# A hybrid mixer block with 32 experts on one core: adaLN sums on VectorE alone, a ninth weight slot, work taken out of the first expert pair, and another order for the last expert pair's down weights

## The chip, the cores and the metric

The kernel runs on one core of one Trainium2 chip. TensorE (PE) does matrix products into PSUM; VectorE (DVE), ScalarE (ACT) and GpSimd (POOL) do elementwise work; SyncE (SP) issues nearly all DMA loads, in the order of its own queue. The metric is device microseconds of one whole run.

## The reference, cut to what matters

One layer on 256 tokens of width 1024, all in float32:

```python
mod = silu(c) @ w_ada + b_ada                         # 1024 x 6144; shift1, scale1, gate1, shift2, scale2, gate2
h = rms_norm(x, g_mix) * (1 + scale1) + shift1
z = h @ w_in                                          # feeds four token mixers and 4 x 1024 merge logits
up_n = y_n @ w_branch[n]                              # y_n: MoBA, GLA, retention, sliding window; 256 wide
mixed = sum_n(sigmoid(merge_logits_n) * up_n) @ w_out
x = x + gate1 * mixed
h2 = rms_norm(x, g_ffn) * (1 + scale2) + shift2
logits = h2 @ w_router + b_router                     # top 4 of 32, softmax over the four
for e in range(32):                                   # every expert's weights are read: 12 MB each
    gu = h2 @ w_gate_up[e] + b_gate_up[e]             # 1024 x 2048
    act = clamped_swiglu(gu)
    y += combine[:, e] * (act @ w_down[e] + b_down[e])  # 1024 x 1024
x = rms_norm(x + gate2 * y, g_final)
```

## The kernel before, in words

**The front.** `ada(s_, j)` (L235) forms one half (512 columns) of one of the six rows of `mod`: two 1 MB loads bring 8 tiles of 128x512; the first four are multiplied by a column of silu(c) on ACT (L249; on POOL, L247, for row 2), added on POOL (L251), and the other four are multiplied and added on DVE (L254). The steps are dealt out one by one among the other work (`slow_step`). `z = h @ w_in` is made in units of 256 columns: `z_unit` splits each float32 weight tile of 128x512 into a high part (ACT, L347) and the rest (DVE, L348), and TensorE multiplies three of the four products of parts (L361, 48 matmuls a unit). The low parts sit in a pool of WP=4 tiles. The last 16 units are the merge units: each also multiplies a mixer's output by a piece of w_branch (`pu`, L809, 12 matmuls), takes a sigmoid, a product (L816) and a sum into `mix` (L817, partly on POOL). The output projection (`pw`, L765) follows; w_out is first multiplied by gate1 on POOL (L774). Then come the logits: x1 is transposed, multiplied by the router (L873, result transposed), copied and turned back by a second set of matmuls (L896); then the top 4 (L905 to L909), the places of the tokens (`pos`), and `gather` (L982 to L1010), which picks each expert's up to 64 tokens by a selection matrix `pm`.

**The experts.** They are taken in pairs, four to a group. `gate_up(e)` reads four 2 MB tiles `wg` (L1067, 64 matmuls of 512 columns), swiglu follows on ACT and DVE, `down(e)` reads two 2 MB tiles `wd` (L1094), and `scatter` multiplies the pair's result back to the tokens' places (`py`, L1104). In pair 0, `down_bias` (L957 to L973: the 32 b_down rows weighted for every token, `pyb`) and the transposes of `spread` (`psm`, L1032, fed by POOL's `pc`, L1024) stand between the two downs. For the last pair, `last_down` loads both experts' w_down by blocks of columns, 256 (three times) and 128 (twice) wide, expert 30's and 31's for each block, and finishes each block at once (`pdl`, L1128; `ol`; `pyl`, L1135; `x_sb`, L1137), so that the final norm is nearly done when the last weights arrive.

**What sets the order.** All loads stand in SP's queue in program order. `slot` deals them out over a ring of 2 MB slots: 5, and 3 more from the third merge branch on; a load waits until its slot's former contents have been read, and everything behind it on SP waits with it. Half slots (1 MB) are dealt by `wtile`. The engines run their own queues in order; a scheduler chose the order in each.

Of the kernel before, what the change touches and what calls it, by code (L numbers as in the profile page):

```python
# [42 lines left out]
def hybrid_block_kernel(ctx, tc, x, c, w_ada, b_ada, g_norm_mix, w_in, w_gla_gate, b_gla_gate, g_gla_norm,  # L43
# [191 lines left out]
    def ada(s_, j):  # L235
        w = []
        for i in range(2):
            t = wtile(f"wada{s_}_{j}{i}").rearrange("p (k f) -> p k f", f=512)
            nc.sync.dma_start(t, w_ada[0, i * 512:(i + 1) * 512, s_ * D + j * 512:s_ * D + (j + 1) * 512].rearrange(
                "(k p) f -> p k f", p=P))  # L240
            w += [t[:, k, :] for k in range(4)]
        acc = acs[s_, j] = mp.tile([P, 512], F32, tag="acs", name=f"acs{s_}{j}", bufs=1)
# [16 lines left out]
    def ada_end(s_, j):
        while slow:  # L260
            slow_step()
        acc = acs.pop((s_, j))
        pt = bank("t", f"pmt{s_}{j}")
        for kk in range(4):
            T.transpose(pt[:, kk * P:(kk + 1) * P], chan(acc, kk) if s_ in (3, 4) else acc[:, kk * P:(kk + 1) * P],
                        ident)
        col = cp.tile([P, 4], F32, tag="ade", name=f"ade{s_}{j}")
        V.tensor_reduce(col, pt.rearrange("p (k r) -> p k r", k=4), AX.X, ALU.add)
        V.tensor_tensor(modT[:, s_, 4 * j:4 * j + 4], col, bT[:, s_, 4 * j:4 * j + 4], ALU.add)
# [1051 lines left out]
```

## Time and profile before

| | us |
|---|---|
| median of 3 runs (lowest, highest) | 1263.29 (1259.78, 1267.72) |
| the profiled execution's own time | 1264.25 |
| its span in the trace | 1262.5 |
| front, up to the first gather matmul | 314.4 |
| from there to the last update of x | 937.6 |
| final norm and output | 10.5 |

Busy over the span: PE 93%, DVE 38%, ACT 16%, POOL 10%. The core moved 469.88 MB, 372 GB/s on average and 428 GB/s in the long middle. A busy PE is modelled from pipelined matmuls, so a high share doesn't say that it ran at its peak; the number of instructions in a stretch tells more.

### The profile page before, as it was taken

How to read it: one execution, taken by the hardware profiler on the slowest of the kernel's cores; microseconds unless marked ns; L12 is line 12 of the kernel's file. 1: busy time of each engine (PE TensorE's matmuls, PEld its weight loads, DVE VectorE, ACT ScalarE, POOL GpSimd, SP SyncE). 2: the span in 40 equal slices, each digit the busy share in tenths (PEclk: the TensorE clock that was granted, in tenths of full speed). 3: DMA queues.
4: the chain of work that ended last, by engine and by line, in shares of the span. 5: the costliest groups of instructions: out<-in, count | busy, mean ns of one | idle time of the engine just before them, and what ended most of it. 6: DMA issues, size and time to landing. Idle time of an engine off the chain costs nothing.

```text
span 1262.5 us, 14878 instructions
## 1 busy us (share of the span) xinstructions
PE 1172.2 (93%) x6204; PEld 567.7 (45%) x6204; DVE 484.4 (38%) x833; ACT 204.8 (16%) x403; POOL 131.2 (10%) x171
## 2 busy tenths in 40 slices
PE   7999999989999999999999999999989998989875
PEld 4778798987333433333333333333323332332224
DVE  3797598986342312222222223222212222132123
ACT  3458355445100000000000000000000000000001
POOL 2332213740000000000000000000000000000001
PEclk9999899999999999999999999999999999999999
DMA  9975369947889999999999999999999999999994
GB/s 324 337 248 201 133 221 341 346 160 276 320 365 396 429 427 429 427 427 428 428 428 428 428 428 428 426 428 427 429 427 428 427 428 428 428 427 428 427 382 145
DMA packets 74730, 469.88 MB, mean 372 GB/s; under 512 B 6425, under 2 KB 27010, under 8 KB 50594
## 3 DMA queue, kind: packets, MB, share of 16 engines
q1 hardware_dynamic: 74034, 467.64, 90.6%
q10 hardware_dynamic: 624, 1.23, 0.3%
q8 instruction: 50, 0.82, 0.3%
q14 instruction: 22, 0.18, 0.0%
HBM read 467.81 MB, written 1.05 MB: 371 GB/s over the span
## 4 chain that ended last, share of the span: by engine, by line
PE 61%; DMA 23%; DVE 10%; issue 2%; ACT 1%; POOL 1%; ACTq 0%; SPq 0%; POOLq 0%; DVEq 0%
DMA wd<-in_w_down_dram 13%; PE ed L1094 13%; PE ea L1067 12%; PE eb L1067 12%; DMA wg<-in_w_gate_up_dram 9%; PE pz_m L361 5%; PE py L1104 4%; PE pg L1000 2%; PE pw L765 2%; PE pu L809 1%; PE pdl L1128 1%; DMA wada<-in_w_ada_dram 1%; PE eat L1081 1%; DVE el L1045 1%; DVE el L1047 1%
## 5 line engine op out<-in xcount | busy, mean ns | idle before, releaser
L1067 PE MATMUL ea<-wg,he 128*64 128x512 f32 x1024 | 284.9, 600 | 8.9 <-DMA wg<-in_w_gate_up_dram 8.7
L1067 PE MATMUL eb<-wg,he 128*64 128x512 f32 x1024 | 283.6, 593 | 0.0
L1094 PE MATMUL ed<-wd,aT 128*64 128x512 f32 x960 | 214.6, 598 | 9.5 <-DMA wd<-in_w_down_dram 8.3
L1041 DVE TENSOR_SCALAR eg<-ea 128x512 f32<-128x512 f32 x32 | 22.1, 692 | 356.6 <-PE ea L1067 352.5
L1043 ACT ACTIVATE es<-eg 128x512 f32<-128x512 f32 x32 | 20.2, 630 | 827.9 <-DVE eg L1041 827.9
L1067 PEld LDWEIGHTS eb<-wg,he 128*64 128x64 f32 x1024 | 80.2, 137 | 146.9 <-issue 146.8
L1067 PEld LDWEIGHTS ea<-wg,he 128*64 128x64 f32 x1024 | 72.9, 137 | 145.6 <-issue 119.4
L1094 PEld LDWEIGHTS ed<-wd,aT 128*64 128x64 f32 x960 | 67.4, 137 | 143.8 <-issue 126.9
L1024 POOL TENSOR_TENSOR pc<-pm,comb 128x128 f32<-128x128 f32 x64 | 23.5, 402 | 685.2 <-PE psm L1032 624.3
L361 PE MATMUL pz_m<-hh,wl_m 128*128 128x256 f32 x256 | 73.3, 286 | 5.9 <-DVE wl_m L348 5.8
L361 PE MATMUL pz_m<-hh,wh_m 128*128 128x256 f32 x256 | 73.6, 287 | 0.0
L361 PE MATMUL pz_m<-hl,wh_m 128*128 128x256 f32 x256 | 72.1, 282 | 0.0
L1106 DVE TENSOR_TENSOR x_sb<-x_sb,py 128x512 f32<-128x512 f32 x60 | 41.3, 688 | 30.3 <-PE py L1104 30.3
L361 PEld LDWEIGHTS pz_m<-hh,wl_m 128*128 128x128 f32 x256 | 49.0, 191 | 8.0 <-DVE wl_m L348 7.7
L1104 PE MATMUL py<-oa,sm 128*128 128x512 f32 x60 | 33.8, 645 | 19.4 <-DVE oa L1098 19.4
L361 PEld LDWEIGHTS pz_m<-hl,wh_m 128*128 128x128 f32 x256 | 49.1, 192 | 0.1
L361 PEld LDWEIGHTS pz_m<-hh,wh_m 128*128 128x128 f32 x256 | 49.0, 191 | 0.3
L1097 DVE TENSOR_TENSOR oa<-ed,late 64x512 f32<-64x512 f32 x15 | 10.2, 683 | 94.6 <-PE ed L1094 94.6
L1097 DVE TENSOR_TENSOR ob<-ed,late 64x512 f32<-64x512 f32 x15 | 10.2, 682 | 91.0 <-PE ed L1094 91.0
L348 DVE TENSOR_TENSOR wl_m<-win_m,wh_m 128x512 fp32r<-128x512 f32 x44 | 42.0, 971 | 7.0 <-ACT wh_m L347 6.9
L1058 PE MATMUL ea<-bgu,ident 32*64 32x512 f32 x128 | 36.5, 612 | 0.0
L1081 PEld LDWEIGHTS eat<-ident,el 128*128 128x128 f32 x128 | 17.6, 205 | 41.0 <-DVE el L1047 39.3
(450 smaller groups left out, 1567.8 us busy)
## 6 DMA issues: line engine op xcount, KB each, us to landing
wg<-in_w_gate_up_dram SPq DMA_DIRECT2D x128, 2048.0 KB, 26.7
wd<-in_w_down_dram SPq DMA_DIRECT2D x60, 2048.0 KB, 27.0
wada<-in_w_ada_dram SPq DMA_DIRECT2D x13, 1024.0 KB, 7.4
win_m<-in_w_in_dram SPq DMA_DIRECT2D x11, 1024.0 KB
win_c<-in_w_in_dram SPq DMA_DIRECT2D x8, 1024.0 KB, 8.2
wada<-in_w_ada_dram SPq DMA_DIRECT2D x12, 512.0 KB, 7.3
wl<-in_w_down_dram SPq DMA_DIRECT2D x5, 1024.0 KB, 28.8
wada<-in_w_in_dram SPq DMA_DIRECT2D x4, 1024.0 KB, 8.1
```

The lines of the kernel that those rows point to most:

```text
L348: V.tensor_tensor(lk, sk, f32(wk), ALU.subtract)
L361: T.matmul(pz[:, b * 256:(b + 1) * 256], l, r, start=(kh == 0 and b == 0 and kk == 0 and i == 0), stop=last and i == 2, skip_group_check=True)
L765: T.matmul(pw[t, hf_], m_[:, kk, t * P:(t + 1) * P], w[:, 0, :], start=(k == 0 and i == 0), stop=(k == KC - 1 and i == 2))
L1000: last_i["pg"] = T.matmul(pg[:, kk * 256:(kk + 1) * 256], chan(n2[:, t, :], k), pm[:, t].rearrange("p e s -> p (e s)"), start=(i == 0), st ...
L1024: G.tensor_tensor(pc[:, t, :, var, i ^ var, :], pv_[:, :, i, :], cv[:, :, i].unsqueeze(2).to_broadcast([P, EB // 2, CAP]), ALU.mult)
L1041: V.tensor_scalar(g, pa, 7.0, None, ALU.min)
L1058: T.matmul(pp_[64 * j:64 * j + 64, :], ident[r:r + NE, r + e:r + e + 1].to_broadcast([NE, CAP]), bgu[r:r + NE, :], start=True, stop=False, ...
L1067: T.matmul(pp_[64 * j:64 * j + 64, :], he[:, k, (e % EB) * CAP:(e % EB + 1) * CAP], w[:, i * DE + j * 512:i * DE + (j + 1) * 512], start=F ...
L1081: T.transpose(pt[:, q * P:(q + 1) * P], cols, ident)
L1094: T.matmul(pd[64 * jj:64 * jj + 64, :], aT[:, k % 4, 64 * (k // 4):64 * (k // 4) + 64], w[k % 4][:, o * 512:(o + 1) * 512], start=(k == 0) ...
L1104: T.matmul(py, s_[:, hf_, t * P:(t + 1) * P], o, start=True, stop=True)
L1106: V.tensor_tensor(yv, yv, py, ALU.add)
```

## The change

1. **adaLN sums.** `ada(s_, i)` takes 512 rows of all 1024 columns (4 KB runs) and does four DVE steps of 128x1024; ACT and POOL do nothing for it.
2. **Splits** are made 1024 elements wide (WP=3), half as many; the sums into `mix` and the low parts of h move from POOL to DVE.
3. **gate1** multiplies the result of the output projection (DVE, four 128x512 products) rather than w_out (POOL).
4. **Logits in one step:** the transposed x1 is the stationary operand, so that logits come out with tokens on partitions; the copy and the second matmuls go.
5. **Slots** are a deque: new slots are taken first. A ninth slot is made after the front; the load of wd0_1 (expert 0's second down tile) goes into it ahead of `gather`. The bias rows b_gate_up are loaded by ACT's queue, in the third merge branch.
6. **Pair 0:** `down_bias` leaves it and is done in four pieces in the pairs of experts 8 to 14; its `spread` and `scatter` come after `gate_up(2)`.
7. **The last pair:** expert 30's w_down comes as two ordinary 2 MB tiles; only expert 31's comes by column blocks, two blocks at a time (512 columns in all, then 256, then 256). All of the blocks' elementwise work is on DVE but one square on ACT.

```diff
-LAST = (256, 256, 256, 128, 128)
-WP = 4
+LAST = ((0, 256), (512, 128), (768, 128))
+WP = 3
...
+    seq = deque([ring] * RING)
+    def add_slots(pool, n):
+        seq.extendleft([pool] * n)
     def slot(name):
...
+        pool = seq[0]
+        seq.rotate(-1)
+        return pool.tile([P, 4096], F32, tag="w", name=name)
...
-    def ada(s_, j):
+    def ada(s_, i):
+        w = load_rows(f"wada{s_}_{i}", w_ada[0, i * 512:(i + 1) * 512, s_ * D:(s_ + 1) * D], D)
...
         def run():
-            for k in range(4):
-                if s_ == 2:
-                    G.tensor_tensor(w[k], w[k], cact[:, k:k + 1].to_broadcast([P, 512]), ALU.mult)
+            for kk in range(4):
+                k = 4 * i + kk
+                if k == 0:
+                    V.tensor_scalar(acc, w[kk], cact[:, k:k + 1], None, ALU.mult)
                 else:
-                    A.activation(w[k], w[k], AF.Copy, scale=cact[:, k:k + 1])
-                if k:
-                    G.tensor_tensor(w[0], w[0], w[k], ALU.add)
+                    V.scalar_tensor_tensor(acc, w[kk], cact[:, k:k + 1], acc, ALU.mult, ALU.add)
                 yield
-            for k in range(4, KC):
-                V.scalar_tensor_tensor(acc, w[k], cact[:, k:k + 1], w[0] if k == 4 else acc, ALU.mult, ALU.add)
-                yield
...
     def out_split(k, hf_):
         if k not in wo:
             wo[k], wo[k + 1] = load_rows(f"wo{k}", w_out[0, k * P:(k + 2) * P, :], 1024)
-            for w in (wo[k], wo[k + 1]):
-                for h in range(2):
-                    c = slice(h * 512, (h + 1) * 512)
-                    G.tensor_tensor(w[:, c], w[:, c], gate1[:, c], ALU.mult)
...
-                (V if bi == 3 else G).tensor_tensor(mv, mv, sg, ALU.add)
+                V.tensor_tensor(mv, mv, sg, ALU.add)
...
         for kk in range(4):
-            T.matmul(pls[t][32 * kk:32 * kk + 32, 0:P], wr2[:, 4 * g + kk, :], xt[:, kk, :], start=(g == 0),
-                     stop=(g == 1))
+            k = 4 * g + kk
+            pl_i[t] = T.matmul(pls[t][:, 0:NE], xt[:, kk, :], wr2[:, k, :], start=(k == 0), stop=(k == KC - 1)).ins
...
+    add_slots(ctx.enter_context(tc.tile_pool(name="r9", bufs=1, side="right")), 1)
     with tc.tile_pool(name="sp", bufs=1, side="right") as sp:
         u = wg_src(0, 3)
         pref[u[0]] = load_wide(*u, pool=sp)
+        u = units[RING + EXTRA]
+        pref[u[0]] = load_wide(*u)
...
+            if late_sc:
+                sm = spread(b, pm)
+                scatter(0, sm[0], *late_sc.pop())
+            if e + 2 == NE:
+                res = last_pair(e, a0, he, sm[r])
+                break
             a1 = gate_up(e + 1, he)
...
             if e == 0:
                 with tc.issue_after(last_i["pm"]):
                     flag_i = combine()
-                down_bias()
-            if sm is None:
+            elif sm is None:
                 sm = spread(b, pm)
             down(e + 1, a1, oa, ob)
+            if e == 0:
+                late_sc.append((oa, ob))
+                continue
             scatter(e, sm[r], oa, ob)
+            if 8 <= e < 16:
+                down_bias(e // 2 - 4)
...
-    def last_down(e, aTs, s_):
+    def last_pair(e, a0, he, s_):
+        gate_up_bias(e + 1)
+        for k in range(6):
+            gate_up_part(e + 1, he, k)
+        ws = fetch(*wd_src(e, 0))
+        for k in range(6, KC):
+            gate_up_part(e + 1, he, k)
+        ws = ws + fetch(*wd_src(e, 1))
...
+        for q, (c, n) in enumerate(LAST):
+            cs = slice(c, c + 2 * n)
             final = q == len(LAST) - 1
+            w = (slot if n == 256 else wtile)(f"wl{q}")[:, 0:2 * KC * n].rearrange("p (k f) -> p k f", f=2 * n)
+            nk = 4 if final else KC
+            for k0 in range(0, KC, nk):
+                nc.sync.dma_start(w[:, k0:k0 + nk, :], w_down[0, e + 1, k0 * P:(k0 + nk) * P, cs].rearrange(
+                    "(k p) f -> p k f", p=P))
```

On SP's queue, at the start of the experts (wg and wd are the 2 MB tiles of gate-up and down weights), before:

```order
L136 DMA wd_0_3565<-in_w_down_dram 128x4096
L953 DMA bgu<-in_b_gate_up_dram 32x512 x4
L136 DMA wg_3_3710<-in_w_gate_up_dram 128x4096
L136 DMA wd_1_3889<-in_w_down_dram 128x4096
L136 DMA wd_0_3969<-in_w_down_dram 128x4096
L136 DMA wd_1_3979<-in_w_down_dram 128x4096
```

and with the change:

```order
L134 DMA wd_0_3168<-in_w_down_dram 128x4096
L134 DMA wg_3_3310<-in_w_gate_up_dram 128x4096
L134 DMA wd_1_3312<-in_w_down_dram 128x4096
L134 DMA wd_0_3522<-in_w_down_dram 128x4096
L134 DMA wd_1_3532<-in_w_down_dram 128x4096
L134 DMA wg_0_3550<-in_w_gate_up_dram 128x4096
```

The four bias loads have left the queue. The order of the weight loads is the same, but wd_1 (the first one) has a slot of its own and needs no release.

On DVE, two of the last merge units (wl are the low parts of the splits: m of w_in, b of w_branch, o of w_out), before:

```order
L348 TENSOR_TENSOR wl_m_1_2_3125<-win_m_00_2978,wh_m_1_2_3124 128x512
L817 TENSOR_TENSOR mix<-mix,msg_0_3058 128x512
L348 TENSOR_TENSOR wl_m_1_3_3141<-win_m_00_2978,wh_m_1_3_3140 128x512
L348 TENSOR_TENSOR wl_b_10_3159<-win_m_21_2783,wh_b_10_3158 128x256
L822 TENSOR_TENSOR ml_3084<-mix,mh_3083 128x512
L348 TENSOR_TENSOR wl_b_11_3163<-win_m_21_2783,wh_b_11_3162 128x256
L348 TENSOR_TENSOR wl_o_3192<-wo_0_3185,wh_o_3191 128x512
L348 TENSOR_TENSOR wl_o_3202<-wo_0_3185,wh_o_3201 128x512
L816 TENSOR_TENSOR msg_1_3156<-pu_1_3166,msg_1_3156 128x512
```

and with the change:

```order
L341 TENSOR_TENSOR wl_m_1_0_2785<-win_m_00_2682,wh_m_1_0_2784 128x1024
L341 TENSOR_TENSOR wl_m_1_1_2813<-win_m_00_2682,wh_m_1_1_2812 128x1024
L811 TENSOR_TENSOR msg_0_2754<-pu_0_2760,msg_0_2754 128x512
L341 TENSOR_TENSOR wl_b_1_2843<-win_m_21_2507,wh_b_1_2842 128x512
L812 TENSOR_TENSOR mix<-mix,msg_0_2754 128x512
L817 TENSOR_TENSOR ml_2776<-mix,mh_2775 128x512
L341 TENSOR_TENSOR wl_o_2868<-wo_0_2865,wh_o_2867 128x1024
L341 TENSOR_TENSOR wl_o_2884<-wo_0_2865,wh_o_2883 128x1024
L811 TENSOR_TENSOR msg_1_2840<-pu_1_2846,msg_1_2840 128x512
```

The same elements go through DVE in wider instructions; on POOL, the multiplications of w_out that stood beside this place are gone.

On PE, the end of the last pair with the change (ea, eb are expert 31's gate-up sums, ed expert 30's down, pdl expert 31's down by blocks):

```order
L1065 MATMUL eb_6711<-wg_2_6736,he_6339 64x512 x2
L1128 MATMUL ed_6760<-wd_0_6746,aT_6708 64x256 x16
L1065 MATMUL ea_6710<-wg_3_6748,he_6339 64x512 x2
L1065 MATMUL eb_6711<-wg_3_6748,he_6339 64x512 x2
L1079 MATMUL eat_6807<-ident,el_6803 128x128 x4
L1128 MATMUL ed_6760<-wd_1_6758,aT_6708 64x256 x16
L1150 MATMUL pdl_6817<-wl_6815,aT_6812 64x256 x16
L1162 MATMUL pyl_0_6836<-oa_6793,sm_1_6607 128x256
L1150 MATMUL pdl_6851<-wl_6849,aT_6812 64x128 x16
```

Before, all gate-up matmuls of expert 31 came first, then the column blocks of both experts in turn; now the first half of expert 30's down stands ahead of expert 31's last gate-up tile, and only expert 31's blocks come at the end.

## Rows read from the trace of the kernel before

**Rows 1.** Busy time by stage; columns in the first row.

```profile
core 0: us, PE busy (x) PEld busy (x) DVE busy (x) ACT busy (x) POOL busy (x), PEclk, DMA share, GB/s
54.00:308.00 254.00, 241.45 (x1809) 218.88 (x1807) 210.20 (x348) 136.24 (x277) 88.94 (x59) 0.97 0.68 249
385.00:1212.00 827.00, 781.10 (x3508) 271.55 (x3508) 204.35 (x315) 34.04 (x57) 17.39 (x48) 1.00 1.01 428
1212.00:1250.00 38.00, 31.45 (x216) 18.03 (x213) 11.70 (x21) 2.56 (x9) 4.78 (x4) 1.00 0.83 268
```

**Rows 2.** The same by 5 us at the start of the experts.

```profile
340.00:345.00 5.00, 5.00 (x24) 1.83 (x22) 0.69 (x1) 0.00 (x0) 0.00 (x0) 1.00 0.27 59
...
370.00:375.00 5.00, 3.43 (x14) 0.90 (x10) 2.67 (x4) 0.00 (x0) 3.15 (x8) 1.00 0.85 360
375.00:380.00 5.00, 5.00 (x17) 1.79 (x19) 2.65 (x5) 0.00 (x0) 1.10 (x3) 0.66 0.00 0
380.00:385.00 5.00, 5.00 (x21) 1.65 (x18) 1.38 (x2) 0.00 (x0) 1.85 (x6) 1.00 0.95 324
```

**Rows 3.** Timeline of SP's queue: start, us, engine, line, operation.

```profile
323.39 8.75 SPq L136 DMA_DIRECT2D wd<-in_w_down_dram  x3
343.09 40.15 SPq L136 DMA_DIRECT2D wg<-in_w_gate_up_dram  x8
```

**Rows 4.** Timeline of PE in the first pair, idle before in brackets.

```profile
366.50 3.02 PE L970 MATMUL pyb<-bdn,cT 32*128 32x512 f32 x6
...
377.63 4.82 PE L1094 MATMUL ed<-wd,aT 128*64 128x512 f32 x17
```

**Rows 5.** Timeline of DVE in the front.

```profile
54.31 3.01 DVE L348 TENSOR_TENSOR wl_sq<-win_c,wh_sq 128x256 fp32r<-128x256 f32 x3 [0.66 <-ACT wh_sq L347]
...
57.78 5.34 DVE L348 TENSOR_TENSOR wl_sq<-win_c,wh_sq 128x256 fp32r<-128x256 f32 x5
...
77.13 3.22 DVE L348 TENSOR_TENSOR wl_gv<-win_c,wh_gv 128x512 fp32r<-128x512 f32 x2
80.27 1.76 DVE L254 SCALAR_TENSOR_TENSOR acs<-wada,cact,acs 128x512 f32<-128x512 f32 x1
81.95 0.68 DVE L348 TENSOR_TENSOR wl_gv<-win_c,wh_gv 128x512 fp32r<-128x512 f32 x1
82.55 0.74 DVE L254 SCALAR_TENSOR_TENSOR acs<-wada,cact,acs 128x512 f32<-128x512 f32 x1
...
267.90 0.41 DVE L348 TENSOR_TENSOR wl_b<-win_m,wh_b 128x256 fp32r<-128x256 f32 x1
```

**Rows 6.** Timeline of POOL there.

```profile
71.67 4.15 POOL L247 TENSOR_TENSOR wada<-wada,cact 128x512 f32<-128x512 f32 x3 [9.17 <-DMA wada<-in_w_ada_dram]
```

**Rows 7.** Timeline of PE: the last pu matmul of four merge units.

```profile
233.58 0.28 PE L809 MATMUL pu<-yh,wl_b 128*128 128x256 f32 x1
...
240.45 0.28 PE L809 MATMUL pu<-yh,wl_b 128*128 128x256 f32 x1
...
248.70 0.28 PE L809 MATMUL pu<-yh,wl_b 128*128 128x256 f32 x1
...
269.19 0.28 PE L809 MATMUL pu<-yh,wl_b 128*128 128x256 f32 x1
```

**Rows 8.** Busy time by 20 us in the front.

```profile
120.00:140.00 20.00, 17.93 (x130) 14.63 (x129) 12.25 (x20) 7.28 (x15) 4.90 (x3) 0.75 0.81 297
```

**Rows 9.** PE's waits from 318 to 1252: us in total, times, longest.

```profile
PE ea L1067 <- DMA wg<-in_w_gate_up_dram: 8.7, 10, 1.3
PE ed L1094 <- DMA wd<-in_w_down_dram: 8.3, 8, 1.2
```

**Rows 10.** Busy time by 4 us at the end.

```profile
1228.00:1232.00 4.00, 4.00 (x25) 2.71 (x25) 0.00 (x0) 0.00 (x0) 0.00 (x0) 1.00 1.10 351
...
1240.00:1244.00 4.00, 3.92 (x41) 2.68 (x38) 2.37 (x4) 0.51 (x2) 1.27 (x1) 1.00 0.69 187
```

**Rows 11.** Timeline of DVE at the end.

```profile
1252.00 0.42 DVE L1137 TENSOR_TENSOR x_sb<-x_sb,pyl 128x256 f32<-128x256 f32 x1 [0.80 <-PE pyl L1135]
```

More of the change, by code (lines that the diff above doesn't have):

```diff
@@ L233, in hybrid_block_kernel @@
     acs = {}
-    def ada(s_, j):
[L236 to L242, printed above, removed]
+    def ada(s_, i):
+        w = load_rows(f"wada{s_}_{i}", w_ada[0, i * 512:(i + 1) * 512, s_ * D:(s_ + 1) * D], D)
+        if i == 0:
+            acs[s_] = mp.tile([P, D], F32, tag="acs", name=f"acs{s_}", bufs=1)
+        acc = acs[s_]
@@ L255, in run, with ada_end @@
                 yield
         slow.append(run())
-    def ada_end(s_, j):
+    def ada_end(s_, i):
         while slow:
             slow_step()
[L262 to L269, printed above, removed]
+        if i == 0:
+            return
+        acc = acs.pop(s_)
+        for j in range(2):
+            pt = bank("t", f"pmt{s_}{j}")
+            for kk in range(4):
+                k = 4 * j + kk
+                T.transpose(pt[:, kk * P:(kk + 1) * P], chan(acc, k) if s_ in (3, 4) else acc[:, k * P:(k + 1) * P],
+                            ident)
+            col = cp.tile([P, 4], F32, tag="ade", name=f"ade{s_}{j}")
+            V.tensor_reduce(col, pt.rearrange("p (k r) -> p k r", k=4), AX.X, ALU.add)
+            V.tensor_tensor(modT[:, s_, 4 * j:4 * j + 4], col, bT[:, s_, 4 * j:4 * j + 4], ALU.add)
@@ L365, in z_unit @@
         pz = bank("z", f"pz_{name}")
-        for kh in range(4):
-            wh, wl = split(tiles[kh // 2][:, 2 * (kh % 2):2 * (kh % 2) + 2, c0:c0 + 256], 2, 256, f"{name}_{kh}", sw)
-            z_part(pz, wh, wl, kh, token)
-            bg()
-            slow_step()
+        for i in range(2):
+            wh, wl = split(tiles[i][:, :, c0:c0 + 256], 4, 256, f"{name}_{i}", sw)
+            for j in range(2):
+                z_part(pz, wh[:, 2 * j:2 * j + 2, :], wl[:, 2 * j:2 * j + 2, :], 2 * i + j, token)
+                bg()
+                slow_step()
         return pz
@@ L857, in out_last @@
         cs = slice(g * 512, (g + 1) * 512)
-        V.tensor_tensor(x_sb[:, t, cs], x_sb[:, t, cs], pw[t, g], ALU.add)
+        tm = mp.tile([P, 512], F32, tag="t2", name=f"gx{t}{g}")
+        V.tensor_tensor(tm, pw[t, g], gate1[:, cs], ALU.mult)
+        V.tensor_tensor(x_sb[:, t, cs], x_sb[:, t, cs], tm, ALU.add)
     def x1_logits(t, g):
@@ L900, in hybrid_block_kernel @@
         rss.append(ssq2[:, t, 3:4])
-    with tc.issue_after(sel_i):
-        pb5 = gate_rows(5, "ab")
-    for t in range(NT):
-        V.scalar_tensor_tensor(lg[:, t, :], pls[t][:, P:P + NE], rss[t], brt, ALU.mult, ALU.add)
+        n2_first(t)
+        V.scalar_tensor_tensor(lg[:, t, :], pls[t][:, 0:NE], rss[t], brt, ALU.mult, ALU.add)
         V.max(mx[:, t, :], lg[:, t, :])
@@ L913, in hybrid_block_kernel @@
     pp_i = T.matmul(pp[:, NE:2 * NE], ustr, mask[:, 1, :], start=False, stop=True, skip_group_check=True).ins
+    with tc.issue_after(mask_i):
+        n2_low(0, slice(0, 256))
     V.scalar_tensor_tensor(pos, pp[:, 0:NT * NE].rearrange("p (t e) -> p t e", t=NT), 1.0, mask, ALU.add, ALU.mult)
-    for q in range(4):
+    for q in range(1, 4):
         for t in range(NT):
@@ L919, in hybrid_block_kernel @@
                 A.activation(n2h[:, t, cs], x_sb[:, t, cs], AF.Copy, scale=rss[t])
-    for t in range(NT):
-        with tc.issue_after(sq_i[NT - 1, 1]):
-            A.activation(scr[:, t, 0:256], x_sb[:, t, 0:256], AF.Copy, scale=rss[t])
-        G.tensor_tensor(n2l[:, t, 0:256], scr[:, t, 0:256], f32(n2h[:, t, 0:256]), ALU.subtract)
     def combine():
@@ L950, in hybrid_block_kernel @@
     comb = epa.tile([P, NT, NE], F32, tag="comb", name="comb")
[L951 to L954 removed]
+    bdn = epa.tile([NE, D], F32, tag="bdn", name="bdn")
     A.dma_start(bdn, b_down[0])
```

241 lines of the change are left out of this document (123 added, 118 removed).

## The prediction, made blind

> **What bounds the kernel now.** I read the stages first. Three matter [rows 1]. From 54 to 308 us (the front) no engine is at its end: PE is busy 241 of 254 us, DVE 210, the DMA engines move 249 GB/s of the 428 that they reach later. From 385 to 1212 the DMA moves a flat 428 GB/s, while PE is busy 781 of 827 us: the weight stream is the bound, PE close behind. From 1212 to 1250 the stream falls to 268 GB/s. So three questions decide: does the front end sooner, does the stream lose less time where the experts begin, and is the end shorter.
>
> Where the experts begin, the view by 5 us shows two holes in the stream [rows 2]: most of 340 to 345 (59 GB/s), and 370 to 385 (360, 0 and 324 GB/s). SP's queue tells why [rows 3]: three `wd` loads go out from 323.39, the next, a `wg`, at 343.09, and the eight from there take 40 us to go out; a load waits until PE has read the slot that comes next. In the second hole PE works on pair 0's `pyb` (3.02 us for six matmuls) and on the rest of its second down, which runs as late as 377.63 to 382.45 [rows 4].
>
> In the front, DVE works beside POOL. A low-part subtraction of 128x256 takes 0.41 us alone [rows 5] (the row at 267.90), but eight of them between 54 and 63 us take 8.35 us, so 1.04 each; two `wl_gv` take 3.22 against 0.68 for one alone, one `acs` 1.76 against 0.74. POOL was at its own products then [rows 6]. In the merge units at 240 to 269, where POOL multiplies w_out, the distance from one unit's last `pu` to the next is 8.25 us for one unit and 20.49 for the two after it, where it was 6.87 just before [rows 7].
>
> **The change, part by part.** The sum is made against the profiled execution, 1264.25 us, which is 1.0 above the median of the three runs.
>
> *POOL's work taken away in the front.* The rows named give back 8.35 - 8x0.41 = 5.1 us (`wl_sq`), 3.22 - 2x0.68 = 1.9 (`wl_gv`) and 1.76 - 0.74 = 1.0 (`acs`): 8 us of DVE time between 54 and 82. Against it, DVE takes over the first four of each sum's eight steps, which ACT and POOL did. A step of 128x1024 does not occur before; it lies between 0.74 us (the price of half its width) and 1.48 (twice that [rows 5]). I take 1.3, since nearly all of a step's time goes with its width. 32 of them are 42 us over the whole front, for 32 narrow ones at 0.74 (24 us) now; in the stretch to 82 us only some four fall, 2 us more. So 6 us of the 8 remain, if PE follows DVE there.
>
> *The merge units.* Three units lose 8.25 + 20.49 - 3x6.87 = 8.1 us against the pace before them. A set of router matmuls lies in there and has to be done anyway, and DVE gets wider but no fewer elements: I take 5. The sums into `mix` (one 128x512 a unit, 0.7 by the `wl_gv` row) come to DVE, which still fits beside 6.87 us of PE.
>
> *The one-step logits and gate1's product.* One turn PE-DVE-PE less before the top 4, one product of 128x512 (0.7) more before it: nothing in sum. The bias loads leave SP's queue, where they stood in front of a load that had a slot; this shows in nothing once the stream runs.
>
> So the **front** gives 6 + 5 = 11 us. Its bounds: 2, if PE's own work fills what DVE gives up; and 18, which is PE's whole idle time (254 - 241.45 = 12.6 [rows 1]) and the 5 us that a granted clock of 0.75 costs in 120 to 140 [rows 8] (a mean of 2.4 GHz and 1.2, half the time each).
>
> *The ninth slot* lets one 2 MB load run before the gather, in idle DMA time, rather than behind the first release: 2.1 MB at 428 GB/s are 4.9 us off the stream. *Pair 0 without bias and scatter* lets PE finish its second down some 8 to 10 us sooner, and the hole of 370 to 385 closes: 0.8 + 5.0 + 1.2 = 7.0 us [rows 2]. The 340 hole stays, since the releases that set it don't move. `down_bias` is done later: four times about 1 us of PE (two of six matmuls in 3.02), in pairs where PE waits for DMA little; hidden or not, the work is as much as before.
>
> *The tail.* 38 us at 268 GB/s are 10.2 MB, 23.8 us at 428; the last transfers run until about 1242.5 (187 GB/s from 1240 to 1244 [rows 10]), 30.5 us. So 6.7 are lost on short runs. With the change, 4.2 MB stay in blocks; at 351 GB/s [rows 10] they lose 2.1 us: 4.6 gained. After the last transfer PE has 9.5 us of work left up to the last `x_sb` at 1252.00 [rows 11]. With two blocks at once the last piece is 256 columns of one expert; all products of the blocks now queue on DVE. I put this lag between 3 and 8 us and take 5: 4.5 gained.
>
> By the stream, the **experts** would give 4.9 + 7.0 + 4.6 + 4.5 = 21 us. But PE bounds it too. All its waits for weights are 8.7 + 8.3 = 17.0 us [rows 9], and the granted clock of 0.66 from 375 to 380 (two thirds of it at 1.2 GHz) costs 1.7 [rows 2]: 19 us is what PE can give back at most. Where two limits stand this close, each makes the other wait in turn; I take 15, with 8 and 20 as ends.
>
> One rule of the Trainium skill speaks against the tail's part: DMA: Bandwidth & Descriptors, in Specifications, has transfers at line rate from 512 bytes on. The trace disagrees: blocks with runs of 1 KB moved at 351 GB/s, below 428 [rows 1, 10]. By the rule the 4.6 us would not come.
>
> **Sum:** 1264.25 - 11 - 15 = **1238 us**. Its own range is 1229 to 1247.
>
> **The rivals.**
>
> *A. The front is PE's* (0.16). For it: PE is busy 95% there. Against it: instructions on DVE that take twice their time, with PE's units 1.4 times as long beside them. Gain 2 + 15: 1247.
>
> *B. PE sets the pace of the experts* (0.12). The stream's lead is then stock in slots that PE can't use: of 19 us it gives back 8. For it: 781 of 827 us busy. Against it: waits for weights in 18 places. 1264 - 11 - 8 = 1245.
>
> *C. Run length is not what slows the tail* (0.07). Then the transfers at the end stay as slow, 4.6 us less gain: 1243.
>
> *D. Slower* (0.06): DVE waits for w_ada. Before, POOL and ACT took the first tiles as they landed, and POOL once stood 9.17 us waiting for one [rows 6] while DVE went on. Now the sum's steps stand in DVE's one queue between the splits that PE needs; a tile that is late holds up all of them. There are 16 such loads of 1 MB. If eight come late by half of 9.17, that is 37 us, and the front's gain is gone with it: 1264 - 15 + 37 = 1286. From 26/16 = 1.6 us a load on, nothing is gained. Against it: DVE is busy 210 of 254 us, so tiles had time to land, and the DMA has room.
>
> Above the forecast's own range lies little else; below it 0.05, where both gains come whole (1264 - 18 - 20 = 1226).
>
> **Chances and range.** The forecast has 0.54. The range takes it, A, B, C and most of the better case: **1225 to 1253**. About 1% (12.6 us) is what a measurement of this kernel tells from no change. Faster by more than that (under 1251): the forecast, C and the better case, most of A and B: 0.84. Within 1%: the rest of A and B, and a small D: 0.10. Slower: 0.06.
>
> **What would show it.** In the changed trace: low parts of 128x256 near 0.41 us everywhere in the front and no POOL row beside them; the last `pu` rows of the late units 7 us apart; the first gather near 303 us; no stretch of 5 us without DMA after the 340 hole; less than 6 us from the last weight's landing to the last `x_sb`. I am wrong if DVE shows idle time that ends with a w_ada transfer, if PE is as long in the front with DVE emptier, or if PE's waits for weights vanish while the stream shows new holes behind slots.

## The result, and the profile after

The changed kernel takes 1231.86 us (median of 4 runs, 1230.69 to 1232.64) beside 1262.19 for the kernel before (4 runs): a ratio of 0.9753, 95% interval 0.9719 to 0.9787. That is 30 us less where 26 were forecast (1238, range 1225 to 1253). The profiled execution took 1232.64 us with a span of 1230.9.

| | before | after | difference | forecast |
|---|---|---|---|---|
| first gather matmul `pg` | 314.4 | 297.7 | -16.7 | -11 |
| from `pg` to the last `x_sb` | 937.6 | 922.6 | -15.0 | -15 |
| of it: from `pg` to the end of the weight stream | 929.3 | 911.8 | -17.5 | -16.5 |
| of it: from there to the last `x_sb` | 8.3 | 10.8 | +2.5 | -4.5 |

By windows of half a microsecond the stream ends at 1243.75 before and at 1209.5 after (the prediction took 1242.5 from windows of 4 us).

**The front.** DVE with the change; columns: start, us, engine, line, operation, idle before in brackets. These rows answer to [rows 5].

```profile
55.40 1.29 DVE L338 TENSOR_TENSOR wl_sq<-win_c,wh_sq 128x512 fp32r<-128x512 f32 x2 [1.69 <-ACT wh_sq L337]
57.35 1.22 DVE L341 TENSOR_TENSOR wl_skv<-win_c,wh_skv 128x1024 fp32r<-128x1024 f32 x1 [0.66 <-ACT wh_skv L340]
...
120.22 1.28 DVE L245 SCALAR_TENSOR_TENSOR acs<-wada,cact,acs 128x1024 f32<-128x1024 f32 x1
```

A low part of 512 columns takes 0.65 us (two in 1.29), one of 1024 takes 1.22: nothing is doubled any more. The new step of 128x1024 takes 1.28 (1.3 was taken), the first of each row's eight 0.75. The last `pu` row of four late merge units, PE with the change, beside [rows 7]:

```profile
225.97 0.28 PE L804 MATMUL pu<-yh,wl_b 128*128 128x256 f32 x1
...
234.15 0.28 PE L804 MATMUL pu<-yh,wl_b 128*128 128x256 f32 x1
...
243.06 0.28 PE L804 MATMUL pu<-yh,wl_b 128*128 128x256 f32 x1
...
250.13 0.28 PE L804 MATMUL pu<-yh,wl_b 128*128 128x256 f32 x1
```

These are units 10 to 13 (counted from 0), 8.2, 8.9 and 7.1 us apart; [rows 7] shows units 9, 10, 11 and 13. From unit 10 to 11 nothing was gained (8.25 before), from 11 to 13 it was 20.49 and is 16.0 now. Busy time by stretch with the change (columns as in [rows 1]):

```profile
54.00:104.00 50.00, 50.00 (x350) 41.88 (x350) 38.95 (x90) 29.89 (x69) 0.00 (x0) 1.00 0.75 279
...
126.00:130.00 4.00, 4.00 (x29) 3.08 (x29) 3.21 (x5) 0.00 (x0) 0.00 (x0) 1.00 0.98 335
130.00:140.00 10.00, 10.00 (x73) 7.91 (x71) 6.99 (x10) 2.69 (x4) 0.00 (x0) 1.00 0.30 114
```

PE has no idle time there, nor from 220 to 270. The largest single gain was not in the forecast's sum, and it lies at 126 to 140. The same two stretches before:

```profile
126.00:130.00 4.00, 2.05 (x18) 1.64 (x16) 4.00 (x9) 0.65 (x2) 1.82 (x2) 1.00 0.11 8
130.00:140.00 10.00, 9.89 (x38) 7.37 (x39) 2.67 (x6) 0.63 (x1) 0.00 (x0) 0.50 1.03 387
```

In ten microseconds PE did 38 matmuls before and does 73 now: its granted clock was at 0.50, the lower of its two levels (1.2 GHz), all that time. What stood ahead of it, in the timelines of POOL, DVE and PE before:

```profile
122.84 5.06 POOL L251 TENSOR_TENSOR win_m<-win_m 128x512 f32<-128x512 f32 x3 [12.48 <-ACT win_m L249]
```

```profile
123.63 1.44 DVE L254 SCALAR_TENSOR_TENSOR acs<-wada,cact,acs 128x512 f32<-128x512 f32 x1
124.99 1.77 DVE L348 TENSOR_TENSOR wl_rg<-win_c,wh_rg 128x512 fp32r<-128x512 f32 x1
126.68 0.49 DVE L654 COPY_PREDICATED glat<-cmask,pgat 128x128 f32<-128x128 int32 x2
127.08 1.37 DVE L254 SCALAR_TENSOR_TENSOR acs<-wada,cact,acs 128x512 f32<-128x512 f32 x1
```

```profile
129.31 0.33 PE L667 MATMUL po_gla<-z_gv,glat 64*64 64x64 f32 x2 [1.59 <-DVE glat L654]
130.11 0.47 PE L667 MATMUL po_gla<-z_gv,glat 64*64 64x64 f32 x2 [0.47 <-DVE glat L654]
```

Three DVE instructions beside POOL's additions took 1.44, 1.77 and 1.37 us for 0.75, 0.68 and 0.75, 2.4 us more in all; so `glat` came late, PE stood idle 1.59 and 0.47 us, and then ran at half clock. From the first `pz_rg` to the first `pz_m` of the merge stage it was 18.6 us before (123.7 to 142.3) and is 10.6 now.

The same happened once more before, in merge unit 6: POOL's additions, `acs` steps of 1.68 us, PE waiting for `wl_m`, and a lower clock. The rows are from the timelines of POOL and PE and from the busy time by stretch:

```profile
195.00 4.40 POOL L251 TENSOR_TENSOR wada<-wada 128x512 f32<-128x512 f32 x3 [2.09 <-ACT wada L249]
...
201.40 0.38 PE L361 MATMUL pz_m<-hh,wl_m 128*128 128x256 f32 x1 [1.75 <-DVE wl_m L348]
...
202.00:204.00 2.00, 2.00 (x11) 2.00 (x11) 2.00 (x3) 0.42 (x1) 1.38 (x1) 0.50 0.81 253
```

That unit's last `pu` came 10.5 us after the one before it, where it is 7.1 now.

**The start of the experts** with the change, by 5 us, beside [rows 2]:

```profile
320.00:325.00 5.00, 5.00 (x26) 1.77 (x23) 1.52 (x3) 0.00 (x0) 0.00 (x0) 1.00 0.25 108
...
350.00:355.00 5.00, 5.00 (x26) 1.70 (x24) 1.38 (x2) 0.00 (x0) 0.00 (x0) 1.00 1.02 436
355.00:360.00 5.00, 5.00 (x26) 1.60 (x24) 0.00 (x0) 0.00 (x0) 0.00 (x0) 1.00 1.04 442
360.00:365.00 5.00, 5.00 (x24) 1.57 (x20) 0.48 (x1) 0.00 (x0) 0.00 (x0) 1.00 0.99 419
```

The first hole is still there (108 GB/s for 59), the second, which would lie at 354 to 368 here, is closed. PE's waits for weights, beside [rows 9]:

```profile
PE ed L1092 <- DMA wd<-in_w_down_dram: 6.4, 6, 1.2
PE ea L1065 <- DMA wg<-in_w_gate_up_dram: 5.4, 6, 1.2
...
PE ed L1128 <- DMA wd<-in_w_down_dram: 1.0, 1, 1.0
```

Together they are 12.8 us where they were 17.0. **The end**, PE and then DVE with the change (beside [rows 11]):

```profile
1200.26 0.73 PE L1079 MATMUL eat<-ident,el 128*128 128x128 f32 x4 [2.21 <-DVE el L1045]
1200.92 5.20 PE L1128 MATMUL ed<-wd,aT 128*64 128x256 f32 x32
1205.96 3.62 PE L1150 MATMUL pdl<-wl,aT 128*64 128x256 f32 x32
1210.11 0.70 PE L1162 MATMUL pyl<-oa,sm 128*128 128x256 f32 x2 [0.54 <-DVE oa L1155]
...
1219.00 0.49 PE L1162 MATMUL pyl<-oa,sm 128*128 128x128 f32 x2 [0.72 <-DVE oa L1155]
```

```profile
1213.50 1.22 DVE L1170 TENSOR_TENSOR res<-x_sb,late 128x1024 f32<-128x1024 f32 x1
1214.75 0.29 DVE L1155 TENSOR_TENSOR oa<-pdl,late 64x128 f32<-64x128 f32 x1
...
1220.29 0.69 DVE L1165 TENSOR_TENSOR x_sb<-x_sb,pyl 128x512 f32<-128x512 f32 x1 [1.03 <-PE pyl L1162]
```

PE waits 2.21 us for expert 31's activation (`el`), and its clock falls once more; the clock with the transfers at the end, by 4 us (beside [rows 10]):

```profile
1200.00:1204.00 4.00, 3.74 (x20) 2.14 (x22) 0.81 (x2) 0.00 (x0) 0.00 (x0) 0.58 0.95 325
1204.00:1208.00 4.00, 4.00 (x40) 2.64 (x38) 1.51 (x4) 0.00 (x0) 0.00 (x0) 0.99 0.75 259
```

So the weights are all there at 1209.5, and PE has only finished the first block's `pdl` then: 10.8 us are left. The fall of the clock is not part of the change: in the traces of experiments 1, 5, 6 and 11, where nothing at the end differs, the same wait of 2.21 us is followed by a clock of 1.00. Experiment 5, PE:

```profile
1209.56 0.63 PE L1082 MATMUL eat<-ident,el 128*128 128x128 f32 x4 [2.21 <-DVE el L1048]
...
1213.98 3.67 PE L1153 MATMUL pdl<-wl,aT 128*64 128x256 f32 x32 [0.18 <-DMA wl<-in_w_down_dram]
```

`pdl` begins 4.4 us after that wait there and 5.7 above, so the fall cost 1.3 us; PE is in time for the first block there, and the lag behind the last weight is still 9.2 to 9.5 us in these four traces.

### The profile page after: what moved, and what is told of

Its sections match the earlier page's. It is cut to its first block, busy times and chain, and to the rows that moved or that the text cites. A ratio compares the mean times of both kernels' runs of the same rounds, so it can differ in the third digit from the quotient of the medians.

```text
span 1230.9 us, 14471 instructions
## 1 busy us (share of the span) xinstructions
PE 1158.8 (94%) x6204; PEld 566.6 (46%) x6204; DVE 452.3 (37%) x764; ACT 177.0 (14%) x293; POOL 36.6 (3%) x105
## 3 DMA queue, kind: packets, MB, share of 16 engines
q10 hardware_dynamic: 816, 1.49, 0.3%
## 4 chain that ended last, share of the span: by engine, by line
PE 64%; DMA 26%; DVE 7%; issue 1%; ACT 1%; POOL 0%; SPq 0%; ACTq 0%; POOLq 0%; DVEq 0%
DMA wg<-in_w_gate_up_dram 19%; PE ea L1065 12%; PE eb L1065 12%; PE ed L1092 11%; DMA wd<-in_w_down_dram 6%; PE pz_m L354 6%; PE py L1102 3%; PE pw L758 2%; PE pg L998 2%; PE pu L804 1%; PE eat L1079 1%; DVE el L1043 1%; DVE el L1045 1%; DVE es L1044 1%; PE pm L274 1%
## 5 line engine op out<-in xcount | busy, mean ns | idle before, releaser
L1065 PE MATMUL ea<-wg,he 128*64 128x512 f32 x1024 | 280.0, 600 | 5.8 <-DMA wg<-in_w_gate_up_dram 5.4
L1065 PE MATMUL eb<-wg,he 128*64 128x512 f32 x1024 | 278.2, 594 | 0.0
L1092 PE MATMUL ed<-wd,aT 128*64 128x512 f32 x960 | 211.5, 595 | 7.6 <-DMA wd<-in_w_down_dram 6.4
L1065 PEld LDWEIGHTS eb<-wg,he 128*64 128x64 f32 x1024 | 78.4, 137 | 147.8 <-issue 147.7
L1065 PEld LDWEIGHTS ea<-wg,he 128*64 128x64 f32 x1024 | 72.1, 137 | 142.2 <-issue 123.7
L1056 PE MATMUL eb<-bgu,ident 32*64 32x512 f32 x128 | 36.5, 612 | 0.0
## 6 DMA issues: line engine op xcount, KB each, us to landing
wd<-in_w_down_dram SPq DMA_DIRECT2D x62, 2048.0 KB, 26.8
```

The source lines that it names most:

```text
L1056: T.matmul(pp_[64 * j:64 * j + 64, :], ident[r:r + NE, r + e:r + e + 1].to_broadcast([NE, CAP]), bgu[r:r + NE, :], start=True, stop=False, ...
L1065: T.matmul(pp_[64 * j:64 * j + 64, :], he[:, k, (e % EB) * CAP:(e % EB + 1) * CAP], w[:, i * DE + j * 512:i * DE + (j + 1) * 512], start=F ...
L1092: T.matmul(pd[64 * jj:64 * jj + 64, :], aT[:, k % 4, 64 * (k // 4):64 * (k // 4) + 64], w[k % 4][:, o * 512:(o + 1) * 512], start=(k == 0) ...
```

## The experiments

The theory after the result: the front gained through POOL's absence (slowed DVE instructions, and a clock fall behind them), the experts through the ninth slot and pair 0, and the tail's order cost what its transfers gained. Each kernel is the changed one with one edit; medians stand against 1231.86. On these chips the kernel before had medians of 1261.6 to 1262.7.

**1. No ninth slot.**

```diff
-    add_slots(ctx.enter_context(tc.tile_pool(name="r9", bufs=1, side="right")), 1)
...
-        u = units[RING + EXTRA]
-        pref[u[0]] = load_wide(*u)
```

> The changed kernel (1231.9 us) without the ninth slot: expert 0's second down tile waits for a ring slot again. Theory (the stream's lead is worth its whole load, 2.1 MB at 428 GB/s): 4.9 us longer, 1236.8, with one hole of about 4 us in the stream near 320 us as in the changed kernel. Rival (PE sets the pace of the experts, a lead is only stock in slots): 1232 to 1233, unchanged.

1236.26 us, +4.4; ratio to before 0.9801 (0.9778 to 0.9825). The 4.9 of the forecast holds: a load's worth of idle DMA time before the gather goes unused. In its trace the stream ends 4.9 us later after `pg` (916.7 for 911.8).

**2. Pair 0 as before** (ninth slot stays): the four `down_bias` pieces, `spread` and `scatter` stand in pair 0 again.

```diff
                     flag_i = combine()
-            elif sm is None:
+                for i in range(4):
+                    down_bias(i)
+            if sm is None:
                 sm = spread(b, pm)
             down(e + 1, a1, oa, ob)
-            if e == 0:
-                late_sc.append((oa, ob))
-                continue
             scatter(e, sm[r], oa, ob)
-            if 8 <= e < 16:
-                down_bias(e // 2 - 4)
```

> The changed kernel with the down bias, the spread and the scatter back in pair 0; the ninth slot stays. Theory (the hole in the stream comes back whole, since the ninth slot only shifts which load waits): 7.0 us longer, 1238.9, with a stretch near 355 to 365 us without DMA. Rival 1 (the ninth slot covers one load of that hole): 2.1 us longer, 1234. Rival 2 (PE sets the pace): up to 1233.

1239.22 us, +7.4; ratio 0.9817 (0.9793 to 0.9841). The forecast's 7.0 holds, and the hole is back (by 5 us):

```profile
350.00:355.00 5.00, 5.00 (x11) 1.28 (x12) 4.00 (x7) 0.00 (x0) 0.00 (x0) 0.69 1.01 429
355.00:360.00 5.00, 5.00 (x18) 1.63 (x16) 1.79 (x4) 0.00 (x0) 0.19 (x1) 0.63 0.20 85
360.00:365.00 5.00, 5.00 (x25) 1.80 (x22) 1.24 (x3) 0.00 (x0) 2.72 (x8) 1.00 0.68 213
```

**3. The tail as before:** `last_down` by blocks of both experts.

```diff
-LAST = ((0, 256), (512, 128), (768, 128))
+LAST = (256, 256, 256, 128, 128)
...
```

> The changed kernel with the last pair as before: both experts' w_down by column blocks of 256 and 128, one at a time. Theory (from the changed trace: the last weight lands earlier, but 11.5 us of chain follow it where there were 9.5): about 3 us longer, 1235. Rival (the prediction's sum, 4.6 for the transfers and 4.5 for the lag): 9 us longer, 1241.

1232.09 us, +0.2; ratio 0.9765 (0.9734 to 0.9797). The new tail is worth nothing that can be measured; neither the 3 us expected nor the rival's 9 came. In this kernel's trace the stream ends 915.5 us after `pg` (3.7 later than after), and the last `x_sb` follows 8.3 us behind it (2.5 less): the transfers gained nearly the 4.6 forecast, and a longer lag gave most of it back (1.3 us of it the clock's fall, which the old tail's trace doesn't have).

**4. POOL busy again in the late merge units,** with additions whose result nobody reads.

```diff
             wh, wl = split(tiles[i][:, :, c0:c0 + 256], 4, 256, f"{name}_{i}", sw)
+            if dummy is not None:
+                for r in range(2):
+                    G.tensor_tensor(dummy.rearrange("p (k f) -> p k f", k=2), f32(wh[:, 0:2, :]), f32(wh[:, 2:4, :]),
+                                    ALU.add)
...
```

> The changed kernel with useless work on POOL: in the last eight merge units, each split is followed by two additions of 128x512 on POOL that nobody waits for (32 in all, some 50 us of POOL). Theory (POOL at work makes DVE's instructions with two operands in SBUF wait): splits of 128x1024 take 2 us and more instead of 1.22 beside them, the units 8 to 9 us instead of 6.9, 1240 to 1248 in all. Rival (what mattered was that sums and gate products on POOL stood in a chain that others wait for): the splits stay at 1.22, 1232 to 1233.

1245.80 us, +13.9; ratio 0.9875 (0.9852 to 0.9899). DVE's instructions between 190 and 308 us here (columns: us, mean ns; idle before):

```profile
L341 DVE TENSOR_TENSOR wl_m<-win_m,wh_m 128x1024 fp32r<-128x1024 f32 x13 | 22.7, 1747 | 8.4 <-ACT wh_m L340 8.4
L817 DVE TENSOR_TENSOR mix<-mix,msg 128x512 f32<-128x512 f32 x11 | 12.2, 1112 | 0.0
...
L816 DVE TENSOR_TENSOR msg<-pu,msg 128x512 f32<-128x512 f32 x11 | 7.5, 680 | 0.0
```

and in the changed kernel, 180 to 290:

```profile
L341 DVE TENSOR_TENSOR wl_m<-win_m,wh_m 128x1024 fp32r<-128x1024 f32 x16 | 19.6, 1227 | 13.1 <-ACT wh_m L340 13.1
...
L812 DVE TENSOR_TENSOR mix<-mix,msg 128x512 f32<-128x512 f32 x12 | 8.3, 688 | 0.0
L811 DVE TENSOR_TENSOR msg<-pu,msg 128x512 f32<-128x512 f32 x12 | 8.2, 687 | 0.0
```

Over a stretch in which POOL works half the time, these kinds take 1.4 and 1.6 times as long; `msg`, which reads one operand from PSUM, takes the same time (680 and 687 ns). So POOL does slow DVE in this place. The 13.9 us are not that alone: ACT waited 7.8 us for POOL to let go of the high parts.

**5. The adaLN sums on ACT, POOL and DVE,** as before.

```diff
...
-                if k == 0:
-                    V.tensor_scalar(acc, w[kk], cact[:, k:k + 1], None, ALU.mult)
...
-                    V.scalar_tensor_tensor(acc, w[kk], cact[:, k:k + 1], acc, ALU.mult, ALU.add)
...
+                    A.activation(w[k], w[k], AF.Copy, scale=cact[:, k:k + 1])
+                if k:
+                    G.tensor_tensor(w[0], w[0], w[k], ALU.add)
...
```

> The changed kernel with the adaLN sums as before (halves of 512 columns; four steps on ACT or POOL with POOL's additions, four on DVE). Theory (POOL's additions slow DVE, PE then stands still long enough for its clock to fall): the first merge matmul comes some 8 us later than at 131.7, with a stretch at 1.2 GHz near 130, the first eleven units lose about 4 more: 1242 to 1244. Rival 1 (contention alone, no fall of the clock): 1235. Rival 2 (the sums don't matter): 1232.

1237.75 us, +5.9; ratio 0.9808 (0.9781 to 0.9834). The late `glat` and the half clock are back (POOL 5.21 us from 121.84, `wl_m` of 128x1024 2.30 us beside it, PE idle 1.49), but for a shorter time:

```profile
130.00:132.00 2.00, 2.00 (x11) 1.93 (x10) 1.15 (x2) 0.00 (x0) 0.00 (x0) 0.50 1.05 385
132.00:134.00 2.00, 2.00 (x13) 1.03 (x12) 0.00 (x0) 0.00 (x0) 0.00 (x0) 0.72 1.06 415
```

The merge stage begins at 137.8 instead of 131.7, but 1.8 us of that stand there already at the first `pz_rg`; from there to the first `pz_m` it is 14.9 us (10.6 with the change, 18.6 before). The 10 to 12 us expected are not borne out by the median. The trace, of the slowest of the four runs (1241.07), has the first gather 9.9 us later.

**6. gate1 on w_out and the sums into `mix` on POOL.**

```diff
+                    G.tensor_tensor(w[:, c], w[:, c], gate1[:, c], ALU.mult)
...
-                V.tensor_tensor(mv, mv, sg, ALU.add)
+                (V if bi == 3 else G).tensor_tensor(mv, mv, sg, ALU.add)
...
```

> The changed kernel with w_out multiplied by gate1 on POOL again, and the sums into mix on POOL in the second and third branch. Theory (POOL beside DVE costs the late merge units what they lost before): 4.5 to 8 us longer, 1236 to 1240, splits of 128x1024 near 1.8 us beside POOL. Rival (the wider splits hide it): 1232 to 1233.

1236.51 us, +4.7; ratio 0.9811 (0.9781 to 0.9841): the term of 5 for the late merge units holds in size. The places differ: in this trace, where POOL's products of w_out lie at 218 to 252, units 10 and 14 lose 2.2 and 1.4 us, not units 12 and 13, which lost before.

**7. Splits of 512 elements,** with POOL still away.

```diff
-WP = 3
+WP = 4
...
-            wh, wl = split(tiles[i][:, :, c0:c0 + 256], 4, 256, f"{name}_{i}", sw)
+            wh, wl = split(tiles[kh // 2][:, 2 * (kh % 2):2 * (kh % 2) + 2, c0:c0 + 256], 2, 256, f"{name}_{kh}", sw)
...
```

> The changed kernel with its splits 512 wide as before (twice as many instructions on ACT and DVE, four tiles of look-ahead). POOL stays without work in the front. Theory (some 90 more instructions on DVE at 0.69 each for two instead of 1.22 for one, 0.15 us a pair; units on PE's 6.9 us pace take most of it in): 1 to 4 us longer, 1233 to 1236. Rival 1 (the width is what is still missing of the 30 us, some 7): 1239. Rival 2: nothing, 1232.

1234.04 us, +2.2; ratio 0.9769 (0.9736 to 0.9802), near the edge of what the runs resolve.

**8. The whole front's elementwise work as before** (5, 6 and 7 together, and h's low parts on POOL); logits, slots, experts and tail as changed.

> The changed kernel with the whole front as before in what DVE, ACT and POOL do: adaLN sums, splits 512 wide, w_out times gate1, the sums into mix and half of the low parts of h on POOL. The one-step logits, the order of slots, the experts and the last pair stay as changed. Theory (each part makes the other worse: narrower splits leave less ahead of PE when POOL holds DVE up, and PE's waits let its clock fall): the front's gain goes whole, 16 to 18 us, 1248 to 1250. Rival (the parts add up, 5.9 + 4.7 + 2.2 by the single runs): 1244 to 1245.

1246.70 us, +14.8; ratio 0.9880 (0.9843 to 0.9917). It lies between the sum of the parts (5.9 + 4.7 + 2.2 = 12.8) and the 16 to 18 that a joint effect would give; the medians don't separate these. In the traces, one execution of each, the first gather comes 9.9, 2.9 and 2.1 us later for the parts and 14.9 for all of them, so there the parts add up. Clock at 130 to 140 us: 0.66.

**9. The tail in another order:** expert 31's transposes behind the second half of `ed`.

```diff
-        aT = act_t(e + 1, swiglu(*gu.pop(e + 1), e + 1, f"{e + 1}"))
+        act = swiglu(*gu.pop(e + 1), e + 1, f"{e + 1}")
+        with tc.issue_after(ed_i):
+            aT = act_t(e + 1, act)
```

> The changed kernel with expert 31's transposes behind the second half of expert 30's down on PE, so that this half runs while swiglu is made. Theory (the end is a chain of PE and DVE behind that wait of 2.2 us, and the fall of the clock after it): 2.5 to 3 us shorter, 1229, no stretch at 1.2 GHz near 1202. Rival 1 (the second tile lands too late to run there): 1232. Rival 2 (only the order moves, the clock still falls): 1230 to 1231.

1232.86 us, +1.0; ratio 0.9778 (0.9755 to 0.9802). PE now started the second half of `ed` at 1199.23 and its clock stayed at 1.00, but DVE did the four products of `ed` ahead of the copy of expert 31's transposes, and `pdl` waited 1.77 us for that copy: the wait moved, it didn't go.

**10. Both at once:** the transposes stand inside the second half of `ed`, so that their copy comes before its products, and the squares and products of a finished block come behind the next block's products.

```diff
         for k in range(KC):
+            if k == 6:
+                with tc.issue_after(ed_i):
+                    aT = act_t(e + 1, act)
...
+            if later:
+                with tc.issue_after(o_i):
+                    later.pop()()
...
+            later.append(rest)
...
```

> The changed kernel with another order at the end: expert 31's transposes stand on PE inside the second half of expert 30's down, its copy on DVE ahead of expert 30's products, and a block's squares and final products behind the next block's products. Nothing is computed otherwise. Theory (behind the last weights the end is a chain of PE and DVE, in which DVE's in-order work stands in the way): the first block's matmuls 1.7 us earlier, 1.2 to 2 us less behind them: 3 us shorter, 1229. Rival (the blocks' weights land just in time for the present order): 1232.

1229.49 us (5 runs), -2.4; ratio 0.9736 (0.9708 to 0.9763): the shortest median of all, against 1231.86 and 1262. PE at the end of this kernel:

```profile
1199.12 1.95 PE L1135 MATMUL ed<-wd,aT 128*64 128x256 f32 x16 [1.29 <-DMA wd<-in_w_down_dram]
1200.99 0.66 PE L1081 MATMUL eat<-ident,el 128*128 128x128 f32 x4
1201.58 1.95 PE L1135 MATMUL ed<-wd,aT 128*64 128x256 f32 x16
1204.46 4.29 PE L1158 MATMUL pdl<-wl,aT 128*64 128x256 f32 x42 [0.93 <-DMA wl<-in_w_down_dram]
```

It waits for weights again, not for DVE, and at 1.00 its 32 `ed` matmuls take 3.90 us, not 5.20. The stream ends at about 1209.3, close to the 1209.5 of the changed kernel, and the last `x_sb` starts at 1217.37: 8.1 us, 2.7 less. Of these, 1.3 are the clock, which stayed up in four other traces too without this edit, and 1.4 are the order of DVE's work: from the first `pdl` to the last `x_sb` it is 12.9 us, where it is 14.3 with the change. In those 12.9 us PE is idle only 0.55: what is left of the lag is PE's own work on the blocks. Against the changed kernel alone the gain is within the scatter of the medians (the two intervals overlap); the trace shows it.

**11. gate2's row matmuls behind the last `ppos`,** to bring the gather forward.

```diff
-    with tc.issue_after(pl_i[1]):
-        pb5 = gate_rows(5, "ab")
...
+    with tc.issue_after(pp_i):
+        pb5 = gate_rows(5, "ab")
```

> The changed kernel with the 16 matmuls that spread gate2 (3.27 us at the end of the logits) behind the last matmul of the tokens' places instead of ahead of it. Theory (they stand in PE's queue in front of the places, for which DVE's mask was ready 1.3 us earlier): 1.3 to 2 us shorter, 1230. Rival (the time is given back at the next hole of the stream): 1232.

1234.41 us, +2.5; ratio 0.9795 (0.9769 to 0.9821): no gain. PE at that place:

```profile
293.78 0.18 PE L912 MATMUL ppos<-mask,ustr 128*128 128x32 bf16 x1 [1.67 <-DVE mask L908]
293.81 3.77 PE L289 MATMUL pb<-ident,modT 128*128 128x128 f32 x16
...
299.29 0.40 PE L998 MATMUL pg<-pm,n2h 128*128 128x256 f32 x1
```

The places came 2.8 us sooner, but the row matmuls, which had filled PE's wait, now stood behind it; they ran at half clock (0.52 from 292 to 298; with the change alone 0.59 from 292 to 296) and still ahead of the gather, which came at 299.29 instead of 297.74.

**12. Slots of the third merge branch taken last,** not first.

```diff
-            add_slots(ctx.enter_context(tc.tile_pool(name="rx", bufs=EXTRA)), EXTRA)
+            seq.extend([ctx.enter_context(tc.tile_pool(name="rx", bufs=EXTRA))] * EXTRA)
```

> The changed kernel with the three new slots of the third merge branch dealt out after the five old ones instead of ahead of them. Theory (the loads for that branch then wait for old slots, the first merge units of the branch come late): 2 to 4 us longer, 1234 to 1236. Rival (the loads have time to land anyway): 1232.

1231.36 us, -0.5; ratio 0.9751 (0.9719 to 0.9783): the order in which those slots are dealt is worth nothing.

**Together.** Undoing front, ninth slot, pair 0 and tail one at a time costs 14.8 + 4.4 + 7.4 + 0.2 = 26.8 us of the 30.3. By ratios, each less 0.9753, they add to 0.0127 + 0.0048 + 0.0064 + 0.0012 = 0.0251, and the whole change is 1 - 0.9753 = 0.0247. Within the scatter, these four parts are the change. The one-step logits and the bias loads on ACT's queue were not tried alone.

## Why the prediction was right, and where its steps were not

**The whole** was right in sign and within its own range, and 6 us short: 2 of them because the sum started from 1264.25 and not from the median of 1262.19, the rest because more came from the front (-16.7 for -11). The 15 from the experts came by another split than the forecast's, so that this number was met by luck. Of the signs that it named, three failed: the gather came at 297.7 and not near 303, the last `pu` rows of the late units were not all 7 us apart (8.2 and 8.9), and the lag was not under 6 us.

**Front, to 82 us (6).** 3.3 us by the first `pz_gv` (78.4 to 75.1). The eight DVE microseconds came back, but PE is busy throughout 54 to 104 now: it follows DVE only as far as its own work allows, which was the condition set. The POOL row of [rows 6] ends at 75.8, ahead of the slowed rows; in the trace its additions go on to 81.5, beside them, and others lie at 53.6 to 62.5.

**Merge units (5).** Right: from unit 10's `pu` on the gain grew from 14.5 to 19.0 us, 4.5, and undoing it cost 4.7, though in other units (experiment 6).

**What the front's sum left out.** 8 us between 124 and 142, and 3.9 in merge units 0 to 10, of which 3.5 are unit 6 and its own fall of the clock. The profile had shown the first as a clock of 0.75 [rows 8]; the prediction put its 5 us into the bound of 18 and not into the sum, since it had not followed the half clock back to what stood ahead of it. Its chain (POOL's additions, doubled DVE instructions, late `glat`, PE idle, half clock) stands in the rows above. Bringing the sums back brought back each link, though only 4.3 of the 8 us; with the whole front's elementwise work back (experiment 8) it was 6.3 of them, and the other 1.7 stay open. The last part went the other way: from unit 15's last `pu` to the first gather it was 20.1 us and is 22.4 now, where the one-step logits and gate1's product were put at nothing. With gate1 back on w_out (experiment 6's trace) it is 20.9, so most of this is the product; PE's clock is 0.59 there with the change (292 to 296).

**Experts, by the stream.** Ninth slot 4.9, measured 4.4; pair 0 7.0, measured 7.4; transfers at the end 4.6, measured 3.7 by one trace. **The lag after the last weight is the step that failed:** "I put this lag between 3 and 8 us and take 5: 4.5 gained". It measured 10.8, 2.5 more than before by the same windows. The term counted the last piece's own work, and not that PE still has most of the three blocks to do when that piece lands: their 14.3 us from the first `pdl` to the last `x_sb` began only 3.5 us before the stream's end. Three things make up the 10.8. The clock's fall after the wait for `el` is 1.3, and it comes in some executions only. Each block's squares and products on DVE, which stood ahead of the next block's `oa`, are 1.4. The other 8.1 remain in experiment 10, where PE is hardly idle; that alone is just above the range of 3 to 8.

**The cap.** The stream's sum of 21 was cut to 15 because PE had only 19 to give. 15.0 came, but not for that reason: PE's waits for weights fell only by 4.2, and the ninth slot and pair 0 paid in full. From the gather to the last `x_sb` PE's idle time fell by 6.0 us (54.8 to 48.8) and its busy time by 9.0 (882.8 to 873.8), and the cap had counted nothing of the latter but one fall of the clock. It was the tail's lag, 7 us off its term, that made 21 into 15.

**The rivals.** A: PE is busy all through 54 to 104 and 220 to 270, as A says, yet the front gained 16.7 and not 2: from 54 us to the gather PE's idle time went from 14.4 to 2.2 us. That is nearly all that the bound of 18 allowed, so the forecast's 11 was too careful. B: a lead of the stream was not lost in the slots, as experiments 1 and 2 show. C: its result for the tail (4.6 less) came about, its cause did not: with fewer short runs the stream ended 3.7 us sooner. The Trainium skill, DMA: Bandwidth & Descriptors, in Specifications, has line rate from 512 bytes on. The packets of the two traces disagree: one of 16 KB took 616 ns, one of 2 KB 87, one of 1 KB 51 and one of 512 bytes 30, so 26.6, 23.4, 20.1 and 17.1 bytes a ns. Run length is not all of it: of the changed kernel's last windows the second, with runs of 1 KB alone, moved 259 GB/s at a DMA share of 0.75, so the engines also stood idle a quarter of the time. D: no DVE wait between 30 and 300 us ends with a w_ada transfer.

## What to carry to other kernels

Follow a lower granted clock back to the idle time ahead of it and to what made that: here 2 us of idle TensorE were followed by ten at half clock. Before shortening the last transfers, add up all the work that the engine using them has left when they land, not that of the last piece; a tail whose compute is behind gains nothing from faster weights. Work given from a slow helper engine to VectorE can be more than free where the two had been slowing each other: VectorE was busy 210 of the 254 us from 54 to 308 before and 179 of the 236 from 54 to 290 with the change, though it took over the work of POOL and part of ACT's.
